# Row sums of the norms: one summed tile and two rounded products with ones in place of fp32 sums on TensorE

## The chip, the cores and the metric

One core of one Trainium2 chip runs the whole program. The metric is the device time of one execution in microseconds (us); runs are compared by their median. Five engines take part: TensorE (PE in the profile, with its weight loads as PEld), VectorE (DVE), ScalarE (ACT), GpSimd (POOL) and SyncE (SP), which issues the transfers.

## The reference

Two transformer blocks on a sequence of 256 tokens of 1024 features, batch 1. Only the normalisations matter here; each of them needs, for each token, a sum over the 1024 features:

```python
def rms_norm(x, g):
    xf = x.astype(jnp.float32)
    y = xf * lax.rsqrt(jnp.mean(xf * xf, axis=-1, keepdims=True) + EPS)
    return (y * g.astype(jnp.float32)).astype(x.dtype)

def layer_norm(x, g, b):
    mu = jnp.mean(xf, axis=-1, keepdims=True)
    var = jnp.mean(jnp.square(xf - mu), axis=-1, keepdims=True)
    y = (xf - mu) * lax.rsqrt(var + EPS)
    ...
```

The first block runs, with a residual after each: feed-forward 0, differential attention, feed-forward 1; then keys and values shared from a norm of their own; feed-forward 2, forgetting attention, feed-forward 3; and a final norm. The second block runs the convolution mixers (with one layer norm inside), cross-attention to a memory of 256 tokens (which has its own norm), and a mixture of experts called PEER. Each is preceded by an rms norm of the running x.

## The kernel before

x stays in SBUF transposed, `xT` [128, 8, 256]: features on the partitions in eight tiles (KT = 8), 256 tokens (T) along the free axis. A sum over features is therefore a sum over partitions and over eight tiles.

**Projections.** Every weight matrix streams through SBUF in pieces of 128x1024. A piece lands in `raw`, ACT rounds it to `whi` (L115), DVE makes the rest `wlo` (L116); there are four `whi`/`wlo` buffers. The activations are split the same way into `hi` and `lo`, and each product is three rounded (fp32r) matmuls into one bank, hi with hi, lo with hi and hi with lo (`mm3`, L147 to L149). One piece is 24 matmuls of 256 columns.

**Norm sums.** `Stat.add` squares a tile on ACT (L182). For most norms POOL adds the first seven squares (`sqa`, L193), and TensorE adds that sum and the eighth square over the partitions with fp32 matmuls against ones (L177), which leaves the sum for each token on the partitions, [128, 2]. With `on_pe=True` (memory, the first x norm, the layer norm) TensorE takes all eight squares one by one. `rstd` makes the root (ACT, L198) and the reciprocal (DVE, L199) on those two columns, and `along_row` (L215, two fp32 products with the identity) spreads the result along the tokens on all partitions, in the bank `pt`. ACT copies it to SBUF (`row_s`, L243).

**The pair.** The eight output tiles of a residual (L426) each feed a square and an unscaled `hi`/`lo` pair (`Norm.add`, L237 and L238). The first two weight pieces after a norm run on these unscaled tiles (`Norm.pair`, 48 matmuls into `mm` and `lg`), since they need no row; L257 multiplies the row in afterwards. In that time `scale` (L270 `nt` on DVE, `hi` on ACT, L275 `lo` on DVE; the form without shift uses L160 and L161) rescales the eight tiles. `fm_pair` then takes the next two pieces, k by k as the scaled tiles become ready.

**Order.** Each engine runs its list in order; a scheduler places what is independent. During feed-forward and attention a background task (ada rows: SP loads `araw`, DVE multiplies and sums it, L358) is spread over the same DVE list. In before.py each boundary between two parts is thus: last residual, row chain, `scale`, with weight splits and background work between them.

## Time and profile before

| | |
|---|---|
| median of 3 runs | 2267.92 us (2267.25 to 2269.08) |
| the profiled execution, own time | 2273.0 us |
| its span in the trace | 2271.2 us |
| PE busy | 2230.7 us, 98% of the span, 16748 matmuls |
| DVE busy | 1739.8 us, 77% |
| ACT busy | 1256.8 us, 55% |
| POOL busy | 75.5 us, 3% |
| mean granted clock | 0.995 |

The span is measured from the first to the last instruction; the execution's own time has 1.8 us around it. A busy share counts all stages alike, so what one boundary costs is to be read from the timeline there. The page counts each fp32 matmul of the program as several entries (the two L177 of one square are four entries).

### The profile page before, as it was taken

The page shows a single profiled execution, that of the slowest core. Times are in us where ns is not written, and L with a number is a line of the kernel's source. Part 1 is how long each engine was busy: PE and PEld are TensorE (multiplying, and loading weights), DVE is VectorE, ACT ScalarE, POOL GpSimd, SP SyncE. Part 2 cuts the span into 40 slices and gives each one's busy share as a digit, 9 for nine tenths or more (in the row PEclk, how much of TensorE's full clock was granted, in tenths as well). Part 3 has the DMA queues.
Part 4 walks back from the last instruction along what each step waited for, and adds up shares of the span by engine and source line. Part 5 has one row for each costly group of instructions (what it writes and reads, how often), then busy time and mean ns, then how long its engine had stood idle before and what let it go on. Part 6 is the DMA issues. An engine that isn't in the chain of part 4 may idle for free.

```text
span 2271.2 us, 42683 instructions
## 1 busy us (share of the span) xinstructions
PE 2230.7 (98%) x16748; PEld 2132.8 (94%) x16748; DVE 1739.8 (77%) x3503; ACT 1256.8 (55%) x2387; POOL 75.5 (3%) x80
## 2 busy tenths in 40 slices
PE   8989999999999999999999999999999999999998
PEld 8989998999999999999999999999999999888886
DVE  7757877977777787765799886899668997666665
ACT  5534487544654457545523555445567776555554
POOL 0000100000100020000100010000000000000000
PEclk9999999999999999999999999999999999999999
DMA  9787744777677763555444463355543434555554
GB/s 361 264 297 297 276 188 161 303 273 294 243 263 301 293 230 129 218 181 183 160 163 167 156 223 110 117 185 185 186 158 140 148 131 158 193 187 186 186 189 153
DMA packets 66185, 467.72 MB, mean 206 GB/s; under 512 B 7704, under 2 KB 7992, under 8 KB 10176
## 3 DMA queue, kind: packets, MB, share of 16 engines
q1 hardware_dynamic: 64608, 461.67, 55.3%
q0 software_dynamic: 1088, 2.81, 0.7%
q8 instruction: 132, 2.16, 0.4%
q14 instruction: 69, 0.57, 0.1%
q10 hardware_dynamic: 288, 0.52, 0.1%
HBM read 462.31 MB, written 2.62 MB: 205 GB/s over the span
## 4 chain that ended last, share of the span: by engine, by line
PE 91%; DVE 3%; ACT 3%; DMA 2%; issue 1%; POOL 0%; DVEq 0%; ACTq 0%; POOLq 0%
PE mm L149 22%; PE mm L147 22%; PE mm L148 22%; PE mm L1172 8%; PE lg L1172 8%; PE lg L1122 2%; PE mm L289 2%; DMA raw<-ffn_in 1%; PE po L177 1%; DVE wlo L116 1%; ACT whi L115 1%; DVE lo L238 0%; DVE lo L275 0%; ACT e L572 0%; PE po L958 0%
## 5 line engine op out<-in xcount | busy, mean ns | idle before, releaser
L115 ACT ACTIVATE whi<-raw 128x1024 fp32r<-128x1024 f32 x696 | 733.9, 1059 | 633.3 <-PE mm L148 401.1
L116 DVE TENSOR_TENSOR wlo<-raw,whi 128x1024 fp32r<-128x1024 f32 x696 | 851.3, 1228 | 296.8 <-ACT whi L115 294.9
L147 PE MATMUL mm<-hi,whi 128*128 128x256 f32 x3144 | 902.0, 287 | 9.8 <-ACT sil L450 9.2
L149 PE MATMUL mm<-hi,wlo 128*128 128x256 f32 x3144 | 894.2, 285 | 1.1 <-DVE wlo L116 0.8
L148 PE MATMUL mm<-lo,whi 128*128 128x256 f32 x3144 | 888.3, 283 | 0.1
L147 PEld LDWEIGHTS mm<-hi,whi 128*128 128x128 f32 x3144 | 597.1, 190 | 13.3 <-ACT sil L450 10.1
L149 PEld LDWEIGHTS mm<-hi,wlo 128*128 128x128 f32 x3144 | 597.9, 190 | 2.5 <-DVE wlo L116 2.2
L148 PEld LDWEIGHTS mm<-lo,whi 128*128 128x128 f32 x3144 | 598.4, 190 | 1.0 <-DVE lo L275 0.3
L149 PE MATMUL mm<-ghi,wlo 128*128 128x256 f32 x704 | 197.4, 280 | 0.0
L147 PE MATMUL mm<-ghi,whi 128*128 128x256 f32 x704 | 197.4, 280 | 0.0
L148 PE MATMUL mm<-glo,whi 128*128 128x256 f32 x704 | 197.4, 280 | 0.0
L358 DVE CUSTOM_DVE_ANT_0 araw<-araw,cb 128x1024 f32<-128x1024 f32 x160 | 190.4, 1219 | 4.3 <-DMA araw<-ada 3.3
L160 ACT ACTIVATE vph<-S 128x128 fp32r<-128x128 f32 x256 | 77.0, 302 | 130.7 <-PE lg L1172 130.6
L148 PEld LDWEIGHTS mm<-glo,whi 128*128 128x128 f32 x704 | 132.7, 188 | 0.0
L147 PEld LDWEIGHTS mm<-ghi,whi 128*128 128x128 f32 x704 | 132.7, 188 | 0.0
L149 PEld LDWEIGHTS mm<-ghi,wlo 128*128 128x128 f32 x704 | 132.6, 188 | 0.0
L161 DVE TENSOR_TENSOR vpl<-S,vph 128x128 fp32r<-128x128 f32 x256 | 73.4, 288 | 43.2 <-PE lg L1172 43.1
L820 DVE SCALAR_TENSOR_TENSOR cfc<-cf,vec,cfc 128x256 f32<-128x256 f32 x240 | 100.6, 502 | 0.0
L1114 DVE TENSOR_SCALAR ohA<-cst,sel 128x128 f32<-128x128 f32 x256 | 82.4, 343 | 21.7 <-PE lg L1122 20.7
L1172 PE MATMUL mm<-whi,vph 128*128 128x512 f32 x256 | 80.4, 395 | 0.2 <-ACT vph L160 0.2
L1172 PE MATMUL lg<-whi,vph 128*128 128x512 f32 x256 | 80.5, 395 | 0.0
L1172 PE MATMUL mm<-wlo,vph 128*128 128x512 f32 x256 | 80.5, 395 | 0.0
(389 smaller groups left out, 3269.1 us busy)
## 6 DMA issues: line engine op xcount, KB each, us to landing
raw<-ffn_in SPq DMA_DIRECT2D x88, 1024.0 KB, 5.0
araw<-ada SPq DMA_DIRECT2D x72, 1024.0 KB, 6.9
raw<-peer_u SPq DMA_DIRECT2D x64, 1024.0 KB, 4.8
raw<-peer_v SPq DMA_DIRECT2D x64, 1024.0 KB, 4.8
raw<-ffn_out SPq DMA_DIRECT2D x44, 1024.0 KB, 4.8
araw<-kv_ada SPq DMA_DIRECT2D x8, 1024.0 KB, 6.9
raw<-w_cf SPq DMA_DIRECT2D x8, 1024.0 KB, 4.8
raw<-w_scx SPq DMA_DIRECT2D x8, 1024.0 KB, 4.8
```

Source lines behind the costliest of these rows:

```text
L115: act.activation(hi[:, :m], r, AF.Copy)
L116: last_split[0] = dve.tensor_tensor(lo[:, :m], r, hi[:, :m], op=ALU.subtract)
L147: pe.matmul(o, a[0], b[0], start=start, stop=False)
L148: pe.matmul(o, a[0], b[1], start=False, stop=False)
L149: pe.matmul(o, a[1], b[0], start=False, stop=stop)
L160: act.activation(pair_hi, src, func, **kw)
L161: dve.tensor_tensor(pair_lo, src, pair_hi, op=ALU.subtract)
L289: pe.matmul(o, p[0][:, k * 128:(k + 1) * 128], h32[:, k, :], start=(k == 0), stop=(k == KT - 1))
L358: dve.tensor_tensor_reduce(out=raw[:, i, :], in0=raw[:, i, :], in1=cb, scale=1.0, scalar=0.0, op0=ALU.mult, op1=ALU.add, accum_out=acc[:, ...
L820: dve.scalar_tensor_tensor(o, cf[:, i, j:j + T], w, o, op0=ALU.mult, op1=ALU.add)
L1114: dve.tensor_scalar(A, iota, sel3[:, 0, t:t + 1], sel3[:, 2, t:t + 1], op0=ALU.is_equal, op1=ALU.mult)
L1172: pe.matmul(acc[t][d], lh, rh[:, d * 512:(d + 1) * 512], start=s0, stop=s1)
```

## The change

Every norm now adds all eight squares to one tile: POOL makes the first six adds, DVE the last (L187). That tile is split into a rounded `sqh` (ACT, L160) and the rest `sql` (DVE, L161), and two fp32r products, `ones_r` with each of them (L171, L172, 256 columns), leave the sum of each token on all 128 partitions at once, in `pt`. Root (ACT, L206) and reciprocal (DVE, L207) then run on the whole 128x256 row in SBUF, which `scale` and the other users read. `along_row` and the copy L243 are gone, and so is `on_pe`. The layer norm's mean takes the same way (`Sum`). The memory norm gets its per-token column back by two transposes. `rstd_after` (the norm of a normed x, before the convolutions) becomes the `of` argument. In the diff as shown blank lines are dropped.

```diff
     xT = xp.tile([128, KT, T], F32, name="xT")
-    ones0 = const.tile([128, 256], F32, name="ones0")
-    ones = ones0[:, 0:128]
+    ones = const.tile([128, 128], F32, name="ones")
+    ones_r = const.tile([128, 128], F32R, name="ones_r")
     eps_c = const.tile([128, 1], F32, name="eps_c")
-    dve.memset(ones0, 0.0)
     dve.memset(ones, 1.0)
+    dve.tensor_copy(ones_r, ones)
     dve.memset(eps_c, EPS)
...
-    class Stat:
-        def __init__(self, on_pe=False):
-            self.ps = bank("po", [128, 2, 128])
-            self.acc = None
-            self.k = 0
-            self.on_pe = on_pe
-        def sum(self, sq, first, last_):
-            for t in range(2):
-                o, b = (self.ps, ones0) if first and t == 0 else (self.ps[:, t, :], ones)
-                pe.matmul(o, sq[:, t * 128:(t + 1) * 128], b, start=first and t == 0,
-                          stop=last_ and t == 1, skip_group_check=True)
+    def over_features(src):
+        hi = work("sqh", [128, T], F32R, bufs=1)
+        lo = work("sql", [128, T], F32R, bufs=1)
+        split_into(hi, lo, src)
+        o = bank("pt", [128, T])
+        pe.matmul(o, ones_r, hi, start=True, stop=False)
+        pe.matmul(o, ones_r, lo, start=False, stop=True)
+        return o
+    class Sum:
+        def __init__(self):
+            self.acc, self.k = None, 0
+        def put(self, ap):
+            self.k += 1
+            if self.acc is None:
+                self.acc = ap
+                return
+            acc = work("sqa", [128, T], bufs=3)
+            (dve if self.k == KT else pool).tensor_tensor(acc, self.acc, ap, op=ALU.add)
+            self.acc = acc
+    class Stat(Sum):
...
             act.activation(sq, ap, AF.Square, scale=scale)
-            self.k += 1
-            if self.on_pe:
-                self.sum(sq, self.k == 1, self.k == KT)
-            elif self.k == KT:
-                self.sum(self.acc, True, False)
-                self.sum(sq, False, True)
-            elif self.acc is None:
-                self.acc = sq
-            else:
-                acc = work("sqa", [128, T], bufs=3)
-                pool.tensor_tensor(acc, self.acc, sq, op=ALU.add)
-                self.acc = acc
-        def rstd(self):
-            r = work("rstd", [128, 2], bufs=3)
-            act.activation(r, self.ps[:, :, 0], AF.Sqrt, scale=1.0 / D, bias=eps_c)
+            self.put(sq)
+        def row(self, r=None, scale=1.0, of=None):
+            r = const.tile([128, T], F32, tag="row", name="row", bufs=1) if r is None else r
+            o = over_features(self.acc)
+            if of is not None:
+                dve.tensor_tensor(r, o, of, op=ALU.mult)
+                dve.tensor_tensor(r, r, of, op=ALU.mult)
+                o = r
+            act.activation(r, o, AF.Sqrt, scale=1.0 / D, bias=eps_c)
             dve.reciprocal(r, r)
+            if scale != 1.0:
+                dve.tensor_scalar(r, r, scale, None, op0=ALU.mult)
             return r
-        def rstd_after(self, r1):
-            r = work("rstd", [128, 2], bufs=3)
-            dve.tensor_tensor(r, r1, r1, op=ALU.mult)
-            dve.tensor_tensor(r, self.ps[:, :, 0], r, op=ALU.mult)
-            act.activation(r, r, AF.Sqrt, scale=1.0 / D, bias=eps_c)
-            dve.reciprocal(r, r)
-            return r
-    def along_row(r):
-        o = bank("pt", [128, T])
-        for t in range(2):
-            pe.matmul(o[:, t * 128:(t + 1) * 128], r[:, t:t + 1].to_broadcast([128, 128]), ident,
-                      start=True, stop=True)
-        return o
...
-        def scaled_by(self, st, r=None, scale=1.0):
-            self.row = along_row(st.rstd() if r is None else r)
-            self.row_s = const.tile([128, T], F32, tag="row", name="row", bufs=1)
-            act.activation(self.row_s, self.row, AF.Copy, scale=scale)
+        def scaled_by(self, st, scale=1.0):
+            self.row = st.row(scale=scale)
             return self
...
                 t = work("nt", [128, T], bufs=3)
-                dve.tensor_tensor(t, oo[:, :T], self.row_s, op=ALU.mult)
+                dve.tensor_tensor(t, oo[:, :T], self.row, op=ALU.mult)
                 if self.b is not None:
...
-        def scale(self, keep=None, r=None):
-            row = self.row if r is None else along_row(r)
+        def scale(self, keep=None):
             for k in range(KT):
...
                 t = work("nt", [128, T], bufs=3) if keep is None else keep[:, k, :]
-                dve.scalar_tensor_tensor(t, xT[:, k, :], self.a[:, k:k + 1], row, op0=ALU.mult, op1=ALU.mult)
+                dve.scalar_tensor_tensor(t, xT[:, k, :], self.a[:, k:k + 1], self.row, op0=ALU.mult, op1=ALU.mult)
                 if self.b is None:
...
     hm = [memp.tile([128, KT, T], F32R, name=n) for n in ("mhi", "mlo")]
-    st = Stat(on_pe=True)
+    st = Stat()
     for k in range(KT):
...
     sync.dma_start(out=cb, in_=bass.AP(tensor=io["c"].tensor, offset=io["c"].offset, ap=[[0, 128], [1, D]]))
-    rm = st.rstd()
+    rm_row = st.row(memp.tile([128, T], F32, name="rm_row"))
     act.activation(cb, cb, AF.Silu)
-    rm_row = memp.tile([128, T], F32, name="rm_row")
-    act.activation(rm_row, along_row(rm), AF.Copy)
+    pt = bank("pt", [128, T])
+    rm = memp.tile([128, 2], F32, name="rm")
+    for t in range(2):
+        pe.transpose(pt[:, t * 128:(t + 1) * 128], rm_row[:, t * 128:(t + 1) * 128], ident)
+        dve.tensor_copy(rm[:, t:t + 1], pt[:, t * 128:t * 128 + 1])
...
-    st = Stat(on_pe=True)
+    st = Stat()
     for k in range(KT):
...
     norm = norm_of("0_sc1", "0_sh1")
-    norm.scale(r=st.rstd())
+    norm.scaled_by(st).scale()
     beside = prepare_bias()
...
     pool.memset(kA[64:66], 1.0)
-    r = st.rstd()
     with tc.tile_pool(name="kvp", bufs=1) as kp:
-        hk = norm.scaled_by(st, r).h
+        hk = norm.scaled_by(st).h
         fg = kp.tile([128, KT, 16], F32, name="fg")
...
+    row = norm.row
     norm = Norm(mod("1_sc1"), mod("1_sh1"), h=norm.h)
-    norm.scale(r=r)
+    norm.row = row
+    norm.scale()
     rate[0] = 0.6
...
-    r1 = st.rstd()
-    r12 = st2.rstd_after(r1)
-    dve.tensor_tensor(r12, r12, r1, op=ALU.mult)
+    rsk = ExitStack()
+    rp = rsk.enter_context(tc.tile_pool(name="rp", bufs=1))
+    r1 = st.row(rp.tile([128, T], F32, name="r1"))
+    norm.row = st2.row(of=r1)
+    dve.tensor_tensor(norm.row, norm.row, r1, op=ALU.mult)
...
         h32 = cp.tile([128, KT, T], F32, name="h32")
-        h = norm.scaled_by(st, r12).h
+        h = norm.h
         cf = cp.tile([128, KT, 288], F32, name="cf")
...
-        pm = bank("po", [128, T])
+        mean = Sum()
         for i in range(KT):
-            pe.matmul(pm, ones, cfc[:, i, :], start=(i == 0), stop=(i == KT - 1))
+            mean.put(cfc[:, i, :])
         mu = cp.tile([128, T], F32, name="mu")
-        act.activation(mu, pm, AF.Copy, scale=1.0 / D)
-        st = Stat(on_pe=True)
+        act.activation(mu, over_features(mean.acc), AF.Copy, scale=1.0 / D)
+        st = Stat()
         for i in range(KT):
...
             st.add(cfc[:, i, :])
-        r = along_row(st.rstd())
+        r = st.row()
         chi = cp.tile([128, KT, T], F32R, tag="phi", name="chi", bufs=2)
...
-        row = along_row(r1)
         for k in range(KT):
-            dve.scalar_tensor_tensor(xT[:, k, :], xT[:, k, :], v("final_g", k), row, op0=ALU.mult, op1=ALU.mult)
+            dve.scalar_tensor_tensor(xT[:, k, :], xT[:, k, :], v("final_g", k), r1, op0=ALU.mult, op1=ALU.mult)
         if tap:
...
         proj_fm(W, "w_mix_out", (mhi, mlo), lambda n, o: residual2(n, o, st, norm), wide=True)
+    rsk.close()
     if tap:
...
             t = ap_.tile([128, 256], F32, tag="qT", name="qT", bufs=4)
-            dve.tensor_tensor(t, o, norm.row_s, op=ALU.mult)
+            dve.tensor_tensor(t, o, norm.row, op=ALU.mult)
             qs[n] = t
```

What the scheduler makes of it is shown at three places. First DVE, from the last residual of feed-forward 0 to the first scaled tile of the attention's norm. L426 (L419 in the changed file) is the residual, L238 (L231) the unscaled `lo`, L270 (L260) `nt`, L275 (L265) the scaled `lo`. Before:

```order
L426 SCALAR_TENSOR_TENSOR xT<-mm,mod_gt_1285,xT 128x256
L116 TENSOR_TENSOR wlo<-raw,whi 128x1024
L238 SCALAR_TENSOR_TENSOR lo<-xT,mod_sc_2248,hi 128x256
L199 RECIPROCAL rstd<-rstd 128x2
L270 SCALAR_TENSOR_TENSOR nt<-xT,mod_sc_2248,pt 128x256 x3
L275 SCALAR_TENSOR_TENSOR lo<-nt,mod_sh_1767,hi 128x256 x3
L270 SCALAR_TENSOR_TENSOR nt<-xT,mod_sc_2248,pt 128x256 x3
L275 SCALAR_TENSOR_TENSOR lo<-nt,mod_sh_1767,hi 128x256
L270 SCALAR_TENSOR_TENSOR nt<-xT,mod_sc_2248,pt 128x256
L116 TENSOR_TENSOR wlo<-raw,whi 128x1024
L275 SCALAR_TENSOR_TENSOR lo<-nt,mod_sh_1767,hi 128x256 x3
```

Of the change:

```order
L419 SCALAR_TENSOR_TENSOR xT<-mm,mod_gt_1292,xT 128x256
L116 TENSOR_TENSOR wlo<-raw,whi 128x1024
L187 TENSOR_TENSOR sqa<-sqa,sq 128x256
L231 SCALAR_TENSOR_TENSOR lo<-xT,mod_sc_2255,hi 128x256
L161 TENSOR_TENSOR sql<-sqa,sqh 128x256
L207 RECIPROCAL row<-row 128x256
L260 SCALAR_TENSOR_TENSOR nt<-xT,mod_sc_2255,row 128x256 x3
L265 SCALAR_TENSOR_TENSOR lo<-nt,mod_sh_1774,hi 128x256 x2
L260 SCALAR_TENSOR_TENSOR nt<-xT,mod_sc_2255,row 128x256
L265 SCALAR_TENSOR_TENSOR lo<-nt,mod_sh_1774,hi 128x256
L260 SCALAR_TENSOR_TENSOR nt<-xT,mod_sc_2255,row 128x256 x2
L265 SCALAR_TENSOR_TENSOR lo<-nt,mod_sh_1774,hi 128x256 x3
L260 SCALAR_TENSOR_TENSOR nt<-xT,mod_sc_2255,row 128x256 x2
```

The last add, the split `sql` and the reciprocal of 256 columns stand in the list where the reciprocal of two columns stood, the add behind the weight split L116. The weight split that stood inside the scaling now follows behind it.

Second DVE, from the last residual of the attention to the first scaled tile of feed-forward 1. L358 (L348) is the background's product. Before:

```order
L426 SCALAR_TENSOR_TENSOR xT<-mm,mod_gt_2653,xT 128x256
L358 ISA araw,acc_gt_4541<-araw,cb 128x1024
L358 ISA acc_gt_4541 128x1
L238 SCALAR_TENSOR_TENSOR lo<-xT,mod_sc_4198,hi 128x256
L199 RECIPROCAL rstd<-rstd 128x2
L116 TENSOR_TENSOR wlo<-raw,whi 128x1024
L270 SCALAR_TENSOR_TENSOR nt<-xT,mod_sc_4198,pt 128x256 x3
L275 SCALAR_TENSOR_TENSOR lo<-nt,mod_sh_3323,hi 128x256 x3
L270 SCALAR_TENSOR_TENSOR nt<-xT,mod_sc_4198,pt 128x256 x3
L116 TENSOR_TENSOR wlo<-raw,whi 128x1024
```

Of the change:

```order
L419 SCALAR_TENSOR_TENSOR xT<-mm,mod_gt_2659,xT 128x256
L348 ISA araw,acc_gt_4546<-araw,cb 128x1024
L348 ISA acc_gt_4546 128x1
L187 TENSOR_TENSOR sqa<-sqa,sq 128x256
L231 SCALAR_TENSOR_TENSOR lo<-xT,mod_sc_4204,hi 128x256
L116 TENSOR_TENSOR wlo<-raw,whi 128x1024
L161 TENSOR_TENSOR sql<-sqa,sqh 128x256
L116 TENSOR_TENSOR wlo<-raw,whi 128x1024
L207 RECIPROCAL row<-row 128x256
L116 TENSOR_TENSOR wlo<-raw,whi 128x1024
L260 SCALAR_TENSOR_TENSOR nt<-xT,mod_sc_4204,row 128x256 x3
```

Three weight splits now stand ahead of the scaling, two of them between `sql` and the reciprocal and between the reciprocal and the first `nt`; before one did, behind the reciprocal.

Third DVE, at the norm of feed-forward 3's output ahead of the convolutions, where two sums are kept (x, and x weighted). `r_13168` is r1, the first row. Before:

```order
L238 SCALAR_TENSOR_TENSOR lo<-xT,gfm,hi 128x256
L199 RECIPROCAL rstd<-rstd 128x2
L205 TENSOR_TENSOR rstd<-rstd 128x2
L206 TENSOR_TENSOR rstd<-po,rstd 128x2
L208 RECIPROCAL rstd<-rstd 128x2
L788 TENSOR_TENSOR rstd<-rstd 128x2
L270 SCALAR_TENSOR_TENSOR h_13184<-xT,gfm,pt 128x256 x3
L161 TENSOR_TENSOR lo<-h_13184,hi 128x256 x3
```

Of the change:

```order
L187 TENSOR_TENSOR sqa<-sqa,sq 128x256
L231 SCALAR_TENSOR_TENSOR lo<-xT,gfm,hi 128x256
L187 TENSOR_TENSOR sqa<-sqa,sq 128x256
L161 TENSOR_TENSOR sql<-sqa,sqh 128x256 x2
L207 RECIPROCAL r_13168<-r_13168 128x256
L203 TENSOR_TENSOR row<-pt,r_13168 128x256
L204 TENSOR_TENSOR row<-row,r_13168 128x256
L116 TENSOR_TENSOR wlo<-raw,whi 128x1024 x2
L207 RECIPROCAL row<-row 128x256
L784 TENSOR_TENSOR row<-row,r_13168 128x256
L260 SCALAR_TENSOR_TENSOR h_13194<-xT,gfm,row 128x256 x3
```

Two reciprocals of 256 columns now follow one another, with two products and two weight splits between them, ahead of the first `h`.

## Rows read from the trace of the kernel before

**Rows 1.** The page: the chain that ended last, by engine, share of the span.
```profile
PE 91%; DVE 3%; ACT 3%; DMA 2%; issue 1%; POOL 0%; DVEq 0%; ACTq 0%; POOLq 0%
```

**Rows 2.** Groups by form, PE: line, engine, out<-in, shapes, count | busy us, mean ns | idle.
```profile
L177 PE MATMUL po<-ones,sq 128*128 128x128 f32 x126 | 18.9, 298 | 0.8 <-ACT sq L182 0.7
...
L215 PE MATMUL pt<-cst,rstd 128*128 128x128 f32 x52 | 8.5, 284 | 1.0 <-DVE rstd L199 1.0
...
L177 PE MATMUL po<-ones,sqa 128*128 128x256 f32 x18 | 5.7, 396 | 2.5 <-POOL sqa L193 2.5
...
L882 PE MATMUL po<-cfc,ones 128*128 128x256 f32 x16 | 3.6, 379 | 0.0
```

**Rows 3.** Timeline, the layer norm: start, us, engine, line, operation, out<-in, count.
```profile
1281.25 3.62 PE L882 MATMUL po<-cfc,ones 128*128 128x256 f32 x16
...
1286.25 4.05 PE L177 MATMUL po<-ones,sq 128*128 128x256 f32 x32
...
1294.00 1.08 DVE L894 TENSOR_TENSOR nt<-cfc,pt 128x256 f32<-128x256 f32 x3
```

**Rows 4.** Windows in the first feed-forward: busy us (count) by engine, then granted clock.
```profile
110.00:117.00 7.00, 7.00 (x60) 6.95 (x59) 1.18 (x2) 0.00 (x0) 0.00 (x0) 1.00 0.87 247
...
117.00:124.00 7.00, 0.19 (x3) 0.03 (x1) 0.32 (x1) 1.41 (x3) 0.00 (x0) 0.86 0.72 190
...
124.00:132.00 8.00, 8.00 (x48) 7.92 (x48) 4.74 (x7) 1.28 (x2) 0.93 (x1) 0.70 0.69 208
```

**Rows 5.** Groups by form, DVE: RECIPROCAL, then plain two-operand work, by width.
```profile
L744 DVE RECIPROCAL sm<-sm 128x2 f32<-128x2 f32 x16 | 2.5, 161 | 1.4 <-ACT e L742 1.1
...
L577 DVE RECIPROCAL rs<-sm 128x4 f32<-128x4 f32 x8 | 1.4, 172 | 0.0
...
L1076 DVE RECIPROCAL gs<-gs 128x8 f32<-128x8 f32 x2 | 0.4, 202 | 0.1
...
L233 DVE TENSOR_TENSOR lo<-mod_sh,hi 128x16 fp32r<-128x16 f32 x5 | 0.9, 173 | 0.3 <-ACT hi L232 0.3
...
L161 DVE TENSOR_TENSOR glo<-pr,ghi 128x256 fp32r<-128x256 f32 x88 | 36.7, 419 | 0.2 <-issue 0.2
```

**Rows 6.** Groups by form, POOL and ACT: adds of squares; the copy of the row.
```profile
L193 POOL TENSOR_TENSOR sqa<-sqa,sq 128x256 f32<-128x256 f32 x45 | 45.7, 1016 | 165.6 <-ACT sq L182 138.7 <-issue 25.8 <-POOL sqa L193 0.7
...
L243 ACT ACTIVATE row<-pt 128x256 f32<-128x256 f32 x8 | 3.1, 385 | 10.3 <-PE pt L215 10.3
```

**Rows 7.** Timeline, DVE, first feed-forward to attention.
```profile
275.24 0.48 DVE L426 SCALAR_TENSOR_TENSOR xT<-mm,mod_gt,xT 128x256 f32<-128x256 f32 x1 [0.55 <-PE mm L149]
...
276.27 1.23 DVE L116 TENSOR_TENSOR wlo<-raw,whi 128x1024 fp32r<-128x1024 f32 x1 [0.55 <-ACT whi L115]
...
279.18 1.26 DVE L270 SCALAR_TENSOR_TENSOR nt<-xT,mod_sc,pt 128x256 f32<-128x256 f32 x3 [1.22 <-ACT row L243]
...
283.79 1.23 DVE L116 TENSOR_TENSOR wlo<-raw,whi 128x1024 fp32r<-128x1024 f32 x1
...
287.25 0.49 DVE L275 SCALAR_TENSOR_TENSOR lo<-nt,mod_sh,hi 128x256 fp32r<-128x256 f32 x1
```

**Rows 8.** Timeline, DVE, attention to second feed-forward.
```profile
399.59 0.47 DVE L426 SCALAR_TENSOR_TENSOR xT<-mm,mod_gt,xT 128x256 f32<-128x256 f32 x1
...
399.99 1.21 DVE L358 CUSTOM_DVE_ANT_0 araw<-araw,cb 128x1024 f32<-128x1024 f32 x1
...
403.06 1.26 DVE L270 SCALAR_TENSOR_TENSOR nt<-xT,mod_sc,pt 128x256 f32<-128x256 f32 x3
```

**Rows 9.** Timeline, DVE, last feed-forward to convolutions.
```profile
1108.17 0.48 DVE L426 SCALAR_TENSOR_TENSOR xT<-mm,mod_gt,xT 128x256 f32<-128x256 f32 x1 [0.60 <-PE mm L149]
...
1113.29 1.26 DVE L270 SCALAR_TENSOR_TENSOR h<-xT,gfm,pt 128x256 f32<-128x256 f32 x3 [1.22 <-ACT row L243]
...
1117.96 1.43 DVE L161 TENSOR_TENSOR lo<-h,hi 128x256 fp32r<-128x256 f32 x4
```

**Rows 10.** Timeline, DVE, the start.
```profile
13.15 2.36 DVE L116 TENSOR_TENSOR wlo<-raw,whi 128x1024 fp32r<-128x1024 f32 x2 [0.46 <-ACT whi L115]
```

## The prediction

> **What bounds the kernel now.** I read the page first: TensorE carries 91% of the chain that ended last, DVE and ACT 3% each, transfers 2% [rows 1]. So microseconds taken off TensorE's list are worth their length, but only where TensorE is not about to wait for something else. The places where it does wait are the boundaries between parts, where a new norm needs its row. There I read the timeline boundary by boundary, with one question: when is the first scaled tile ready (L270), when the last (L275), and what stands between residual and row on DVE's list. The forecast is a replay of that list with the changed order, at each boundary, until the next weight piece after the scaled pair can run.
>
> **What leaves TensorE.** L177 and L215 at 128 columns stand 126 + 18 + 52 = 196 times on the page's count; 24 entries of L177 (one first entry of two for each of 12 groups of sums) and the 16 of L882 have 256 columns [rows 2]. In the layer norm 32 entries of L177 took 4.05 us, 0.127 each, and 16 of L882 3.62 us, 0.226 each [rows 3]. 196 x 0.127 + 40 x 0.226 = 33.9 us. A rounded matmul of 256 columns takes 7.00 / 60 = 0.117 us [rows 4]; 26 of them and four transposed entries come in, 3.5 us. If everything else were hidden, the kernel would be 30.4 us faster. That is the upper bound of the gain.
>
> **The price of the new row chain.** The expensive newcomer is the RECIPROCAL on 128x256, which no row of before shows. On 2, 4 and 8 columns it takes 161, 172 and 202 ns: 5.5 and 7.5 ns for each further element, where a subtraction goes from 173 ns on 16 columns to 419 on 256, 1.0 ns for each [rows 5]. Lower bound: it behaves as the subtraction, 0.42 us. Upper: 202 + 248 x 7.5 = 2.06 us. I take 6.25 ns, 1.75 us, because all three rows of the same operation show the steep slope. The other steps: last add and `sql` 0.42 each [rows 5], `sqh` and the root 0.39 each by the copy of the row [rows 6], two products 0.12 each. Serially 0.42 + 0.39 + 0.42 + 0.12 + 0.39 + 1.75 = 3.5 us, and some 0.05 to 0.1 us between engines. The Trainium skill, "VectorE: DVE Perf Modes", section "First, the fixed hardware budget", says that the reciprocal is an iterative divide with a repeat count of 8, and its table has the engine at 0.96 GHz. If that is eight cycles for each element, it gives an estimate of 2.1 us, and the sum below would be some 3 us higher; the rows' 7.5 ns lean that way.
>
> **Feed-forward 0 to attention: +1.6.** Before, the residual ends at 275.72, L116 holds DVE from 276.27 to 277.50, the first scaled tile starts at 279.18 and the last `lo` ends at 287.74 [rows 7]. Of the change, the add stands behind L116: 277.5 to 277.85; `sqh` to 278.35, `sql` to 278.85, products, root to 279.75, reciprocal to 281.5. The scaling starts 2.3 us later. The L116 that stood inside it (283.79, 1.23 [rows 7]) now stands behind, so the last `lo` is only 1.2 later. But that weight split is what the third piece waits for: it ends at about 290.2, where TensorE finished the scaled pair near 288.5 before. Some 48 x 0.117 = 5.6 us of unscaled matmuls cover the chain; what the pair loses of L177 and L215 (1.7 us) makes its cover end earlier and gains nothing here, because the scaling sets the end.
>
> **Attention to feed-forward 1: +3.2.** Residual and background L358 stand as before (399.59, 399.99, to 401.20 [rows 8]). Then add, `lo`, L116, `sql`, L116, reciprocal, L116, each 1.23 for the splits: first scaled tile at about 407.4 instead of 403.06 [rows 8]. One split leaves the scaling again (-1.1): +3.2, with TensorE idle for about 3.5 us.
>
> **Four more boundaries of this pattern**, replayed alike: feed-forward 1 to keys and values, with two L358 in the chain, +2.2; feed-forward 2 to forgetting attention, +1.3; that to feed-forward 3, +1.2 (there TensorE waited before for POOL's last add, and no longer does); cross-attention to PEER, where nothing stands on DVE's list, -0.5. Keys and values to feed-forward 2 loses its second L215, -0.4. The cross-attention norm scales nothing, 0.
>
> **Feed-forward 3 to convolutions: +4.4.** Two sums, and the second row needs the first. Before, residual at 1108.17, scaled tiles from 1113.29, the last `lo` ends at 1119.39 [rows 9]. Now a reciprocal, two products, two L116 (their `whi` waits for buffers that the pair frees) and a second reciprocal: first tile at about 1120.1, 6.8 later; that the scaling has fewer waits of its own and the next splits are already made gives some 2.4 back. TensorE would idle some 6 us. **The clock, +2.2.** In feed-forward 0 it ran 60 matmuls in 7.00 us, then worked 0.19 us of 7.00, and then made only 48 in 8.00 at a mean granted clock of 0.70 [rows 4]: 48 x 0.117 = 5.6, so 2.4 us lost to the lower of the two levels, 1.2 GHz. I charge that once, behind the longest new wait.
>
> **Layer norm: -3.9.** L882 (3.62), L177 (4.05) and four entries of L215 (4 x 0.127) go, 8.2 us; four products, 0.5, come. The squares now take six POOL adds of 1.02 [rows 6], which TensorE must await where it summed each square as it came: about 3.2 us more waiting, and 0.6 for two splits. -8.2 + 0.5 + 3.2 + 0.6 = -3.9. The mean's adds follow tiles that the convolution makes one by one and stay hidden.
>
> **Start: +3.8.** The memory norm's squares were summed as they landed; now six POOL adds follow one another, and the `sql` and the long reciprocal stand among the first weight splits (13.15, 2.36 for two [rows 10]). Those slip by about 2.3 us, the x norm's by a little more; L177 x32 and two L215 leave TensorE. Between 0 (all under transfers) and 5.5.
>
> **Sum.** 3.8 + 1.6 + 3.2 + 2.2 - 0.4 + 1.3 + 1.2 + 4.4 + 2.2 - 3.9 - 0.5 = +15.1 us. The profiled execution took 2273.0, 1.8 of it outside the span, and stands 5.1 above the median of 2267.9; with the change it would take 2288, and the median 2283.
>
> **The rivals.**
> *The chain is hidden.* The pair's cover (5.6 us) holds a chain of 3.5, the scheduler's order costs nothing, and TensorE's saving counts. For it: 91% of the chain is TensorE's. Against it: the scaling, eight tiles at roughly 1 us each, ended after the pair already, at 287.74 [rows 7], so its start decides. All hidden gives 2237.5, half of the boundaries 2253. Chance 0.12.
> *The reciprocal is cheap*, 0.42 us. Then each of seven boundary chains (eight reciprocals) and the start are about 1.3 shorter, 9 x 1.3 = 12, and the convolution boundary's idle falls too short for the clock, 2.2: +1, or 2269, no change. Chance 0.12.
> *The clock falls at every new wait.* TensorE would idle 2 to 4 us at two more boundaries and in the layer norm. At 2.2 to 2.4 each: +5 to +7, 2288 to 2290; with the upper price of the reciprocal (0.3 x 9) up to 2293. Chance 0.22. The Trainium skill, "TensorE: Matmul & The Clock Gate", section "HAM oscillation", describes a kernel that re-throttles at every wait between groups; the row after the idle 7 us agrees, and rows for waits of 3 us are missing.
> *The start is absorbed*: the first stage may be bound by transfers, so +3.8 becomes 0, 2279. That lies inside the likeliest case.
>
> **How the numbers follow.** The likeliest, replay with the 1.75 us reciprocal, has 0.54: 2283, and 2276 to 2288 with its own bounds. A measurement of this kernel tells 0.2%, 4.5 us, from no change, so faster is below 2263.4 and slower above 2272.5. Faster gets the hidden chain, 0.12; same the cheap reciprocal and a little of the likeliest, 0.13; slower 0.75. The range 2260 to 2295 leaves out most of the hidden chain and a little above.
>
> **What would show it.** RECIPROCAL L207 at 1.6 to 2.1 us; L260 first at a boundary 2 to 4 us later after the residual than L270 was; new idle time of TensorE before scaled tiles, the longest, about 6 us, ahead of the convolutions with a lower clock behind it; from the mean's end to the scaled layer norm fewer microseconds of TensorE. It is wrong if L207 takes near 0.4 us, if TensorE's waits at the boundaries are no longer than before, or if the weight splits between the steps turn out to start earlier than I let them.

## The result and the profile after

The changed kernel took 2293.02 us in the median of 4 runs (2292.02 to 2295.68), the kernel before 2268.30 beside it: ratio 1.0106, 95% interval 1.0094 to 1.0118. That is 24.7 us slower where 15.1 were forecast; it lies inside the range, near its upper end. The profiled execution took 2295.68, 2.7 above the median; that of before stood 5.1 above its own, so the traces differ by 22.7 us where the medians differ by 24.7.

The page of the changed kernel: the span, busy time by engine, and the chain that ended last.

```profile
span 2293.9 us, 42338 instructions
PE 2216.1 (97%) x16540; PEld 2113.5 (92%) x16540; DVE 1770.9 (77%) x3532; ACT 1260.2 (55%) x2391; POOL 99.2 (4%) x104
PE 87%; DVE 5%; ACT 4%; issue 2%; DMA 1%; POOL 0%; DVEq 0%; SPq 0%; ACTq 0%; POOLq 0%
```

TensorE's busy time fell by 14.6 us (2230.7 before), the span grew by 22.7. So some 37 us of new idle time stand on the engine that bounds the kernel, and its share of the chain fell from 91% [rows 1] to 87%, where DVE's and ACT's rose.

The new row chain, groups by form of the changed kernel (busy us, mean ns of one, then the idle time ahead):

```profile
L207 DVE RECIPROCAL row<-row 128x256 f32<-128x256 f32 x10 | 17.5, 1748 | 4.0 <-ACT row L206 4.0
L187 DVE TENSOR_TENSOR sqa<-sqa,sq 128x256 f32<-128x256 f32 x12 | 6.3, 527 | 10.3 <-POOL sqa L187 9.7 <-ACT sq L195 0.6
L161 DVE TENSOR_TENSOR sql<-sqa,sqh 128x256 fp32r<-128x256 f32 x13 | 5.5, 421 | 1.9 <-ACT sqh L160 1.6
L206 ACT ACTIVATE row<-pt,eps_c 128x256 f32<-128x256 f32 x9 | 4.2, 471 | 8.4 <-PE pt L172 8.4
L171 PE MATMUL pt<-sqh,ones_r 128*128 128x256 f32 x13 | 4.8, 371 | 12.6 <-ACT sqh L160 12.2
```

The reciprocal takes 1.748 us, as the slope of [rows 5] gave. The last row holds 12.2 us in which TensorE stands before the first of the two products: 4.16 at the start, 3.77 in the layer norm, where the forecast had such a wait, and 1.34 to 1.47 at three boundaries, which I had not counted. There the product lies in the list among the unscaled matmuls, and those behind it wait too.

First boundary, feed-forward 0 to attention, DVE's timeline of the changed kernel:

```profile
276.45 0.48 DVE L419 SCALAR_TENSOR_TENSOR xT<-mm,mod_gt,xT 128x256 f32<-128x256 f32 x1 [0.47 <-PE mm L149]
277.49 1.23 DVE L116 TENSOR_TENSOR wlo<-raw,whi 128x1024 fp32r<-128x1024 f32 x1 [0.55 <-ACT whi L115]
278.63 0.42 DVE L187 TENSOR_TENSOR sqa<-sqa,sq 128x256 f32<-128x256 f32 x1
...
279.53 0.43 DVE L161 TENSOR_TENSOR sql<-sqa,sqh 128x256 fp32r<-128x256 f32 x1
280.96 1.75 DVE L207 RECIPROCAL row<-row 128x256 f32<-128x256 f32 x1 [1.00 <-ACT row L206]
282.75 1.28 DVE L260 SCALAR_TENSOR_TENSOR nt<-xT,mod_sc,row 128x256 f32<-128x256 f32 x3
...
288.63 0.90 DVE L265 SCALAR_TENSOR_TENSOR lo<-nt,mod_sh,hi 128x256 fp32r<-128x256 f32 x2
...
290.17 1.22 DVE L116 TENSOR_TENSOR wlo<-raw,whi 128x1024 fp32r<-128x1024 f32 x1
```

The residual stands 1.21 us later than in [rows 7] (276.45 against 275.24). Less that shift, the reciprocal starts at 279.75, the scaling at 281.54 and the weight split behind it at 288.96: all three within 0.1 us of the replay. The last `lo` ends 0.6 us later than before, where the replay had 1.2.

Second boundary, attention to feed-forward 1, DVE's timeline:

```profile
402.90 0.47 DVE L419 SCALAR_TENSOR_TENSOR xT<-mm,mod_gt,xT 128x256 f32<-128x256 f32 x1
...
406.64 1.21 DVE L116 TENSOR_TENSOR wlo<-raw,whi 128x1024 fp32r<-128x1024 f32 x1
407.78 1.74 DVE L207 RECIPROCAL row<-row 128x256 f32<-128x256 f32 x1
409.44 1.15 DVE L116 TENSOR_TENSOR wlo<-raw,whi 128x1024 fp32r<-128x1024 f32 x1
410.52 1.26 DVE L260 SCALAR_TENSOR_TENSOR nt<-xT,mod_sc,row 128x256 f32<-128x256 f32 x3
```

The first scaled tile comes 7.62 us after the residual's start, 3.47 before [rows 8]: 4.15 later, 4.3 in the replay. What the replay had not priced stands behind it. Windows of the changed kernel, at this boundary and ahead of the convolutions (busy us and count of PE, PEld, DVE, ACT, POOL, then the granted clock, the transfers' share and GB/s):

```profile
406.00:412.00 6.00, 2.79 (x22) 2.59 (x21) 6.00 (x9) 3.46 (x6) 0.00 (x0) 0.93 0.57 218
412.00:420.00 8.00, 8.00 (x46) 7.85 (x46) 8.00 (x21) 2.61 (x6) 0.00 (x0) 0.63 0.32 132
1126.00:1133.50 7.50, 1.35 (x10) 1.14 (x9) 7.29 (x11) 3.19 (x5) 0.00 (x0) 0.85 0.40 140
1133.50:1140.00 6.50, 6.50 (x37) 6.32 (x37) 6.50 (x19) 4.26 (x9) 0.00 (x0) 0.64 0.13 53
```

TensorE ran at the lower of its two levels, 1.2 GHz, for part of the stretch behind each of these waits. At 0.117 us a matmul, 46 would take 5.4 of the 8.00 us and 37 would take 4.3 of 6.50: 2.6 and 2.2 us. I had charged the second and left the first to a rival.

Ahead of the convolutions, DVE's timeline, and under it TensorE's first matmul on scaled tiles:

```profile
1120.32 0.48 DVE L419 SCALAR_TENSOR_TENSOR xT<-mm,mod_gt,xT 128x256 f32<-128x256 f32 x1 [0.58 <-PE mm L149]
...
1124.96 1.75 DVE L207 RECIPROCAL r<-r 128x256 f32<-128x256 f32 x1
...
1127.68 2.36 DVE L116 TENSOR_TENSOR wlo<-raw,whi 128x1024 fp32r<-128x1024 f32 x2
1129.96 1.75 DVE L207 RECIPROCAL row<-row 128x256 f32<-128x256 f32 x1
...
1132.20 1.28 DVE L260 SCALAR_TENSOR_TENSOR h<-xT,gfm,row 128x256 f32<-128x256 f32 x3
```

```profile
1133.18 0.80 PE L147 MATMUL mm<-hi,whi 128*128 128x256 f32 x2 [6.15 <-ACT hi L160]
```

Less the shift of 12.15 us, the first tile stands at 1120.05 (1120.1 in the replay), and the wait is 6.15 us.

The layer norm, POOL's timeline and then TensorE's:

```profile
1306.38 2.02 POOL L187 TENSOR_TENSOR sqa<-sq 128x256 f32<-128x256 f32 x1 [6.26 <-ACT sq L195]
1308.47 4.81 POOL L187 TENSOR_TENSOR sqa<-sqa,sq 128x256 f32<-128x256 f32 x5
```

```profile
1314.24 0.39 PE L171 MATMUL pt<-sqh,ones_r 128*128 128x256 f32 x1 [3.77 <-ACT sqh L160]
```

Six adds end at 1313.28, then one on DVE and the rounding; TensorE stands for 3.77 us in front of its product. Behind this wait, too, the granted clock fell. The first row below is the stretch from the product on; the second is the same stretch of e11, a kernel of the next section in which TensorE does not wait here:

```profile
1314.20:1322.00 7.80, 7.75 (x52) 7.76 (x53) 4.80 (x9) 4.18 (x5) 0.00 (x0) 0.78 0.38 134
1310.90:1318.70 7.80, 7.80 (x68) 7.80 (x67) 6.61 (x10) 6.43 (x8) 0.00 (x0) 1.00 0.76 271
```

At 0.117 us a matmul, 52 would take 6.1 of the 7.75 us: some 1.7 us are lost, at a granted clock of 0.78 against 1.00.

**Where the time went, by stage.** For each instruction of DVE and ACT that both traces have (same tiles, same place in the sequence) I took the difference of its end times; the median over the 14 us that end a stage says how late the kernel is there, and the difference of two such medians what the stage cost. All in us against the trace of the kernel before; the columns e1 to e12 belong to the next section.

```
stage                      forecast after   e1    e2    e3    e7    e9   e10   e11   e12
start and ff 0                 3.8    1.7   1.1   1.7  -2.2  -2.4  -4.6  -4.1   0.0   2.9
ff 0 to attention              1.6    1.6   0.2   7.9   2.9   0.5   0.7   1.4   1.6   0.6
attention to ff 1              3.2    3.8   0.6   8.5   4.7   0.0   1.8   3.6   2.8   2.2
ff 1 to k/v to ff 2            1.8    1.4   2.1   6.9   8.2   0.3   0.7   1.0   1.4   2.9
ff 2 to forgetting att.        1.3    2.9   3.0   8.7   5.0   1.6  -0.7   2.9   3.0   3.1
that to ff 3                   1.2    0.9  -0.1   6.8   2.2   0.1   2.2   2.0   0.9   1.7
ff 3 to convolutions           6.6    7.9   3.5  14.9   8.4   1.4   0.0   7.9   7.8   1.9
convolutions, layer norm      -3.9   -1.1   3.0   0.1   3.9   2.8   0.0  -0.1  -6.7   4.5
cross-attention norm           0.0    0.3  -0.9   8.4  -0.8  -0.5   0.3  -0.8   0.3   0.7
cross-attention to PEER       -0.5    2.8  -0.2   4.5   3.1   1.1   1.0   0.7   1.0  -0.1
sum                           15.1   22.3  12.3  68.5  35.4   4.9   1.4  14.4  12.2  20.3
without the first row         11.3   20.6  11.1  66.8  37.6   7.3   6.0  18.5  12.2  17.4
```

The first row is no measure of the change: e9 leaves the start as before and stands 4.6 us earlier there. From the second boundary on, stages that are alike in two kernels mostly agree within a few tenths. The exceptions are attention to feed-forward 1 (3.8 in the changed kernel, 2.8 in e11) and cross-attention to PEER (2.8 and 1.0). The code there is the same, and so are TensorE's waits (3.21 and 3.19 us, 1.09 and 1.10); what differs is the granted clock behind them. Rows of the changed kernel, then of e11, behind the second of these waits:

```profile
1455.50:1459.00 3.50, 3.12 (x14) 3.15 (x15) 2.80 (x13) 1.24 (x4) 0.00 (x0) 0.51 0.60 201
1447.20:1450.70 3.50, 3.10 (x26) 3.13 (x27) 3.31 (x16) 1.26 (x4) 0.00 (x0) 1.00 0.68 204
```

12 matmuls fewer are some 1.4 us. So a stage that holds such a wait is known to 1 or 2 us from one trace, not better.

### The profile page after: what moved, and what is told of

The parts are those of the page before. It is cut to its first block, busy times and chain, and to the rows that moved or that the text cites. A ratio compares the mean times of both kernels' runs of the same rounds, so it can differ in the third digit from the quotient of the medians.

```text
span 2293.9 us, 42338 instructions
## 1 busy us (share of the span) xinstructions
PE 2216.1 (97%) x16540; PEld 2113.5 (92%) x16540; DVE 1770.9 (77%) x3532; ACT 1260.2 (55%) x2391; POOL 99.2 (4%) x104
## 4 chain that ended last, share of the span: by engine, by line
PE 87%; DVE 5%; ACT 4%; issue 2%; DMA 1%; POOL 0%; DVEq 0%; SPq 0%; ACTq 0%; POOLq 0%
PE mm L149 21%; PE mm L147 21%; PE mm L148 21%; PE mm L1168 8%; PE lg L1168 8%; PE lg L1118 2%; PE mm L279 2%; DVE wlo L116 1%; ACT whi L115 1%; DMA raw<-ffn_in 1%; DVE cfc L816 1%; DVE araw L348 0%; POOL sqa L187 0%; DVE lo L231 0%; DVE row L207 0%
## 5 line engine op out<-in xcount | busy, mean ns | idle before, releaser
L116 DVE TENSOR_TENSOR wlo<-raw,whi 128x1024 fp32r<-128x1024 f32 x696 | 850.0, 1225 | 285.7 <-ACT whi L115 283.8
L348 DVE CUSTOM_DVE_ANT_0 araw<-araw,cb 128x1024 f32<-128x1024 f32 x160 | 190.9, 1221 | 3.1 <-DMA araw<-ada 2.8
L160 ACT ACTIVATE vph<-S 128x128 fp32r<-128x128 f32 x256 | 77.2, 302 | 131.8 <-PE lg L1168 131.7
L161 DVE TENSOR_TENSOR vpl<-S,vph 128x128 fp32r<-128x128 f32 x256 | 73.3, 288 | 43.6 <-PE lg L1168 43.5
L1168 PE MATMUL lg<-whi,vpl 128*128 128x512 f32 x256 | 80.6, 395 | 0.0
```

Of the source, the lines that this page charges most:

```text
L116: last_split[0] = dve.tensor_tensor(lo[:, :m], r, hi[:, :m], op=ALU.subtract)
L160: act.activation(pair_hi, src, func, **kw)
L161: dve.tensor_tensor(pair_lo, src, pair_hi, op=ALU.subtract)
L348: dve.tensor_tensor_reduce(out=raw[:, i, :], in0=raw[:, i, :], in1=cb, scale=1.0, scalar=0.0, op0=ALU.mult, op1=ALU.add, accum_out=acc[:, ...
L1168: pe.matmul(acc[t][d], lh, rh[:, d * 512:(d + 1) * 512], start=s0, stop=s1)
```

## The experiments

Two theories stood against each other. One: the chain of the row on DVE, above all the reciprocal of 256 columns, sets the start of the scaled tiles. The other: the chain is covered, and the time goes to the order of the weight splits or to squares on POOL. Medians in us; before is 2268.1 to 2269.2 beside all of them.

**e1, without the reciprocal.**

```diff
-            dve.reciprocal(r, r)
+            dve.tensor_scalar(r, r, 0.0, 0.25, op0=ALU.mult, op1=ALU.add)
```

> The changed kernel, but the reciprocal of the 128x256 row (1.75 us) is replaced by one multiply and add that sets the row to 0.25, so the normalisation is left out. Theory (the row chain on DVE sets the start of the scaled tiles): each of eight boundary reciprocals gives back 1.4 us where the scaling is late, 8 x 1.4 = 11, the start about 1, and the idle 6 us ahead of the convolutions falls under 4, so its lower clock goes, 2: 2277 to 2281 us. Rival (the order of the weight splits and the squares on POOL cost the time, the reciprocal lies behind them): 2289 to 2293 us.

Measured 2284.35, ratio 1.0065 (1.0048 to 1.0082). The reciprocals are worth 8.7 us of the 24.7 by the medians, 9.5 by the stages. The seven stages at boundaries together gave back 12.2 (1.4 + 3.2 - 0.7 - 0.1 + 1.0 + 4.4 + 3.0), near the theory's 11 and 2, but the layer norm got 4.1 us worse, so the sum stayed short of the expectation. TensorE waited 6.12 us there, as DVE took up the subtractions, behind weight splits, 4.0 us after ACT had begun to write the mean (1.7 in the changed kernel). Ahead of the convolutions the wait fell from 6.15 to 2.16 us, but the lower clock did not go: 0.72 in the stretch 1124 to 1130 us.

**e2, the reciprocal three times.**

```diff
             dve.reciprocal(r, r)
+            dve.reciprocal(r, r)
+            dve.reciprocal(r, r)
```

> The changed kernel with the reciprocal taken three times (1/(1/(1/x))), 3.5 us more in each of the 12 row chains. Theory: 8 boundary chains, each fully exposed, 28 us, the layer norm 3.5, and a lower clock behind more of the waits, 2 to 8: 2325 to 2333 us. Rival (hidden): under 2305 us.

Measured 2342.01, ratio 1.0324 (1.0306 to 1.0341), 49 us more than the changed kernel and above even the theory's 2325 to 2333. The first five boundaries lost 4.7 to 6.3 us more than in the changed kernel for 3.5 us of added chain; behind the longer waits the clock was lower. Windows of e2 from the pair of the first boundary on:

```profile
276.00:286.00 10.00, 6.73 (x55) 6.32 (x53) 7.86 (x10) 4.66 (x7) 2.47 (x8) 0.95 0.69 272
286.00:296.00 10.00, 6.65 (x33) 6.51 (x33) 10.00 (x24) 3.87 (x9) 0.00 (x0) 0.54 0.31 108
```

In the second window 33 matmuls took 6.65 us, 0.20 each, at a granted clock of 0.54. The layer norm took 1.2 us of it (0.1 against -1.1), so its reciprocal is mostly covered; the cross-attention norm, free with one, cost 8.4.

**e3, the chain ahead of the splits.** The third and fourth split after a norm are queued behind the reciprocal.

```diff
-            dve.reciprocal(r, r)
+            hold[:] = [dve.reciprocal(r, r), 2]
...
+            hold[1] -= 1
+            with after(hold) if -2 <= hold[1] < 0 else nullcontext():
+                last_split[0] = dve.tensor_tensor(lo[:, :m], r, hi[:, :m], op=ALU.subtract)
```

> The changed kernel with the third and fourth weight split after a norm, and so the background products, queued on DVE behind the row's reciprocal. Theory: at attention to feed-forward 1 two splits (2.4 us), at feed-forward 1 to keys and values one product of the background (1.2), ahead of the convolutions two splits (2.4) leave the chain; the splits come later by as much, and half of it is lost again to the next piece: 2287 to 2290 us. Rival (the sum of DVE's work between residual and last scaled tile decides, not its order): 2292 to 2295 us.

Measured 2313.18, ratio 1.0202 (1.0185 to 1.0219), 20 us more than the changed kernel. Both expectations fell. TensorE's waits of the changed kernel and then of e3 for `lo` and `wlo`, by the weight loads:

```profile
L148 PEld LDWEIGHTS mm<-lo,whi 128*128 128x128 f32 x3144 | 600.5, 191 | 4.9 <-DVE lo L265 1.9
L149 PEld LDWEIGHTS mm<-hi,wlo 128*128 128x128 f32 x3144 | 600.1, 191 | 4.0 <-DVE wlo L116 3.4
```

```profile
L151 PEld LDWEIGHTS mm<-lo,whi 128*128 128x128 f32 x3144 | 601.4, 191 | 6.6 <-DVE lo L268 4.2 <-DVE lo L164 1.4
L152 PEld LDWEIGHTS mm<-hi,wlo 128*128 128x128 f32 x3144 | 601.0, 191 | 4.5 <-DVE wlo L118 4.2
```

The held splits landed behind the reciprocal: one ahead of the first scaled tile at each of the first two boundaries, two ahead of the convolutions, and a second one at the first boundary between the first `nt` and the first `lo`. There they delay the scaled tiles, and the pieces came later besides. The splits that stood in the gaps of the chain, which I had priced as waits, were not a cost that a better order removes in this way. What makes up all 20 us was not taken apart.

**e4, two columns again but for the second row ahead of the convolutions.** The edit is like that of e7 below, but the second row ahead of the convolutions, which needs the first, keeps the wide way. The kernel also left out the factor of 1/16 of the cross-attention norm's row.

> The changed kernel with root and reciprocal on two columns again: the one summed tile goes unsplit through two fp32 products (four entries), root and reciprocal on 128x2, then the spread along the row and a copy to SBUF as before. Only the second row ahead of the convolutions keeps the wide way. Theory: split (0.8) and long reciprocal (1.6) go, spread and copy with their hand-overs come (1.2), so each of 8 chains is about 1.2 us shorter and the clock ahead of the convolutions stays: 2279 to 2283 us; still above the kernel before, because the last add stands on DVE behind a weight split. Rival (the saved TensorE entries count where the chain is short): 2262 to 2268 us.

Measured 2280.82, ratio 1.0058 (1.0041 to 1.0075), within the theory's figure. By its trace, taken as in the table, it lost 9.5 us behind the first row of the table, 7.3 of them at the one boundary that kept a wide row, with one wide reciprocal.

**e5, the layer norm the old way; e6, the start the old way.** In each the old `Stat` with its fp32 sums stands beside the new one, under the name `OldStat`.

```diff
-        mean = Sum()
+        pm = bank("po", [128, T])
         for i in range(KT):
-            mean.put(cfc[:, i, :])
+            pe.matmul(pm, ones, cfc[:, i, :], start=(i == 0), stop=(i == KT - 1))
...
-        st = Stat()
+        st = OldStat(on_pe=True)
```

> The changed kernel with the layer norm's mean and sum of squares taken the old way (16 entries of L882, 32 of L177, rstd, spread). In the traces the changed layer norm gave back 1.2 us where the prediction had 3.9. If the trace is read rightly: 1 to 2 us slower than the changed kernel, 2294 to 2295 us. If the 3.9 was right and another stage hid it: 2296 to 2298 us.

> The changed kernel with the memory norm and the first x norm taken the old way (each square on TensorE). The prediction gave the start 3.8 us; the traces show TensorE 5.4 us late at 90 us and 3.0 at 145, behind a wait for transfers. If what is left behind that wait counts: 3 us faster than the changed kernel, 2290 us. If the transfers set the time there anyway: 2292 to 2294 us.

e5: 2293.3, ratio 1.0111 (1.0094 to 1.0128), no difference that these runs can tell; by the stages it stands within 0.4 us of the kernel before there, against -1.1, so the new way gained about 1 us and not 3.9. e6: 2300.0, ratio 1.0136 (1.0119 to 1.0153), 7 us slower, on neither expectation. Its trace has the boundaries of the changed kernel (20.7 without the first row) and one long wait in feed-forward 0, which ACT's timeline names:

```profile
110.60 1.06 ACT L116 ACTIVATE whi<-raw 128x1024 fp32r<-128x1024 f32 x1 [14.75 <-DMA raw<-ffn_in]
```

ACT idles 14.75 us until a weight piece has landed, and TensorE behind it. Where such waits fall differs between all the kernels here, those with the same start too, so what the change costs at the start stays open.

**e7, two columns in every norm.**

```diff
+            po = bank("po", [128, 2, 128])
+            for t in range(2):
+                pe.matmul(po[:, t, :], self.acc[:, t * 128:(t + 1) * 128], ones, start=True, stop=True)
...
+            act.activation(c, o, AF.Sqrt, scale=1.0 / D, bias=eps_c)
+            dve.reciprocal(c, c)
...
-            o = over_features(self.acc)
...
-            act.activation(r, o, AF.Sqrt, scale=1.0 / D, bias=eps_c)
-            dve.reciprocal(r, r)
...
+            act.activation(r, along_row(self.cols() if c is None else c), AF.Copy, scale=scale)
```

> All norms with one summed tile and two fp32 products, root and reciprocal on two columns, also ahead of the convolutions, where the earlier kernel of this kind still had two wide reciprocals and lost 5.8 us by its trace. Theory (the wide reciprocal is what costs): that boundary falls to about +1, so 2270 to 2277 us, of the size of the kernel before. Rival (the last add on DVE costs there as much as the reciprocal): 2278 to 2281 us.

Measured 2275.14, ratio 1.0028 (1.0018 to 1.0037). The boundary ahead of the convolutions fell from 7.9 to 1.4 us, as the theory has it. The expectation speaks of two wide reciprocals in e4, but its trace has one: leaving the first row's wide chain out took 0.6 us off there (7.9 to 7.3), the second row's 5.9. 17.9 of the 24.7 us are gone; only one summed tile, its add on DVE, and the layer norm's new sums are left.

**e8, the kernel before with the start's squares on POOL.**

```diff
-    st = Stat(on_pe=True)
+    st = Stat()
```

> The kernel before, with the memory norm and the first x norm summed on POOL as its other norms are. In the trace of the two-column kernel the start was 2.9 us earlier than before. If that comes from the squares that leave TensorE: 2264 to 2266 us; if from the order of the first weight splits alone: 2267 to 2269 us.

Measured 2273.1, ratio 1.0020 (1.0010 to 1.0030): not faster, though the squares there left TensorE's list but for one sum and the last; on neither expectation.

**e9, the wide reciprocal alone.** In the kernel before, at six norms:

```diff
+            if r is None:
+                c = work("rstd", [128, 2], bufs=3)
+                act.activation(c, st.ps[:, :, 0], AF.Copy)
+                act.activation(self.row_s, along_row(c), AF.Sqrt, scale=1.0 / D, bias=eps_c)
+                dve.reciprocal(self.row_s, self.row_s)
...
```

> The kernel before with one part of the change alone: at six norms (five with scaled tiles, and the cross-attention's) the raw sums are spread along the row first, and root and reciprocal run on 128x256; sums, adds and the other norms stay as they were. Theory (the wide reciprocal on DVE delays the scaled tiles): 5 x 1.6 = 8 us plus the clock at one or two waits, 2276 to 2281 us beside a before of 2268. Rival (it is hidden behind the unscaled pair): 2268 to 2270 us.

Measured 2274.45, ratio 1.0024 (1.0015 to 1.0033), 5.5 us, between the two: 8 or more by the theory, at most 2 by the rival. One operation of 1.75 us in place of 0.16 costs 1.1 us on average at each of the five boundaries with scaled tiles when sums and adds stay as they were.

**e10, without the split.**

```diff
-        hi = work("sqh", [128, T], F32R, bufs=1)
-        lo = work("sql", [128, T], F32R, bufs=1)
-        split_into(hi, lo, src)
...
-        pe.matmul(o, ones_r, hi, start=True, stop=False)
-        pe.matmul(o, ones_r, lo, start=False, stop=True)
+        pe.matmul(o, ones, src, start=True, stop=True)
```

> The changed kernel with the summed tile unsplit: one fp32 product with ones (four entries or their like on TensorE) in place of sqh, sql and two rounded products. Theory (the chain on DVE and ACT sets the time): 0.42 + 0.39 and two hand-overs leave each of 8 boundary chains, TensorE gets 0.6 more in its covered time: 1 us each, 2284 to 2287 us. Rival (the splits lie beside other work and TensorE's 13 x 0.6 counts): 2293 to 2300 us.

Measured 2289.87, ratio 1.0098 (1.0084 to 1.0112), 3.2 us less than the changed kernel, between the two expectations, and the intervals overlap. By the stages 2.1 behind the first row, as much as the last boundary alone has, where the granted clock stayed at 1.00 in e10.

**e11, the layer norm's squares added on DVE.**

```diff
-        st = Stat()
+        st = Stat(dve)
...
-            (dve if self.k == KT else pool).tensor_tensor(acc, self.acc, ap, op=ALU.add)
+            (dve if self.k == KT else self.eng).tensor_tensor(acc, self.acc, ap, op=ALU.add)
```

> The changed kernel with the layer norm's seven adds of squares on DVE (0.42 each) in place of six on POOL. In the changed kernel TensorE waits 3.9 us for the first of the two products there. Theory (that wait is for POOL's adds, 1.0 us each): DVE takes 6 x 0.42 = 2.5 of work beside the subtractions that it makes anyway (8 x 0.35), the sum is ready about 2 us earlier and the wait falls to some 2 us: 2290 to 2292 us, and by position in the trace 2 us less in this stage. Rival (the wait is for the squares on ACT and the table load): no difference in this stage, 2292 to 2294 us.

Measured 2287.37, ratio 1.0078 (1.0064 to 1.0092), 5.7 us less than the changed kernel, and 5.6 less in this stage, nearly three times what the theory had: the whole wait of 3.77 us went, not a part of it, and with it the lower clock behind it. TensorE's product in e11, without a wait:

```profile
1310.95 0.28 PE L171 MATMUL pt<-sqh,ones_r 128*128 128x256 f32 x1
```

**e12, e7 with the last add on POOL.**

```diff
-            (dve if self.k == KT else pool).tensor_tensor(acc, self.acc, ap, op=ALU.add)
+            pool.tensor_tensor(acc, self.acc, ap, op=ALU.add)
```

> The kernel with all norms on two columns (2275 us), with the last add on POOL too. Theory (what it still loses against the kernel before is the last add, which queues behind a weight split on DVE): POOL's add takes 1.0 us instead of 0.42 but waits for nothing, so at the boundaries where a split stands ahead (0.5 to 1.2 us of waiting) it is even or 0.5 us better each: 2271 to 2275 us. Rival (the length of the add itself counts): 0.6 us more at each of 8 boundaries, 2278 to 2281 us.

Measured 2288.84, ratio 1.0083 (1.0070 to 1.0097), 13.7 more than e7. The theory fell; the rival's sign is right, its size too small. POOL's add of 1.0 us stands behind the add before it on the same engine, where DVE's took 0.42; and at three boundaries where e7 has a granted clock of 1.00, e12 has 0.72 to 0.74 over some 6 us.

## Why the prediction was right, and where its sizes were off

**The upper bound of the gain** was no gain: TensorE's busy time fell by 14.6 us, not by 30.4 (in part because matmuls at the lower clock take longer), and came back as waits. The page's busy shares could not show that; the timelines did.

**The price of the chain** held: 1.748 us against 1.75, 6.2 ns for each element beyond eight. That it fits so closely is luck: slopes of 5.5 and 7.5 ns allowed 1.57 to 2.06. The upper bound of 2.06 was too high. So was the estimate of 2.1 us from the Trainium skill, "VectorE: DVE Perf Modes", section "First, the fixed hardware budget"; the measurement decides.

**The replay of DVE's list** held to 0.2 us at the three boundaries shown above. e1, e2, e7 and e9 change only the chain's length or form, and the time follows. So the mechanism stands, and the boundary to the attention cost 1.6 us as forecast.

**The clock was mis-sized**, and it is the largest term that was. It was charged once, 2.2 us ahead of the convolutions. It fell at three more places: 2.6 us at attention to feed-forward 1, some 1.7 in the layer norm and some 1.4 at cross-attention to PEER, by the windows above. All three had stood only with the rival, which had +5 to +7 us for two more boundaries and the layer norm, and 5.7 came: it was the better forecast. Only its "every" is wrong, and the length of the last wait does not decide alone. Behind waits of 1.12, 2.07 and 1.07 us (the first boundary, keys and values, feed-forward 3) the changed kernel has a granted clock of 1.00, but behind 1.09 us at PEER it has 0.51. At keys and values, the changed kernel after 2.07 us and e1 after 2.14:

```profile
606.00:616.00 10.00, 8.97 (x67) 8.30 (x68) 10.00 (x26) 6.63 (x16) 0.00 (x0) 1.00 0.01 2
601.30:608.00 6.70, 6.47 (x40) 6.27 (x41) 6.70 (x22) 3.90 (x8) 0.00 (x0) 0.75 0.01 2
```

Attention to feed-forward 1 still came out at 3.8 for 3.2; what gave the rest back was not taken apart.

**Layer norm: -3.9 was wrong, -1.1 measured.** The terms that failed are the clock, put at nothing there, the splits, and to a lesser part the wait. The first product waits 3.77 us where I had 3.2; `sql` of the mean, behind a weight split on DVE, holds TensorE for 1.12 where I had 0.6 for all splits; and the lower clock costs some 1.7. -8.2 + 0.5 + 3.8 + 1.1 + 1.7 = -1.1. e11, which moves the adds of the squares to DVE, takes the wait and the clock away, and -8.2 + 0.5 + 1.1 = -6.6 stands beside its measured -6.7. The wait itself is not six equal adds of 1.02 us: the first took 2.02 us beside DVE's subtractions, the last four 0.72 each, and the three buffers of the squares let ACT go only as fast as POOL.

**The mean's adds do not stay hidden from DVE.** In the changed kernel five of DVE's eight `cfc<-cf,vec` products run beside one of POOL's adds of the mean for most of their time, and these five take 0.81 to 0.88 us. In e5, which sums the mean on TensorE, all eight take 0.41 to 0.42. Rows of the changed kernel and of e5 (ns of the shortest, the median and the longest):

```profile
L814 DVE TENSOR_SCALAR cfc<-cf,vec x8: 404/818/883, 1142.5 to 1263.5; 128x256 f32<-128x256 f32 x8
L875 DVE TENSOR_SCALAR cfc<-cf,vec x8: 406/411/421, 1140.2 to 1259.5; 128x256 f32<-128x256 f32 x8
```

DVE's last tiles of the convolution, compared as in the table, are 1.6 us later than TensorE's list ahead of them, and not later in e5. What of that reaches the end was not separated.

**Cross-attention to PEER: -0.5 was wrong, +2.8 measured.** Some 1.4 us of it is the lower clock, which e11 does not have there: its 1.0 is what the rest costs. For that rest I priced the chain and not the splits behind it, which I had priced at the first boundary. Before, two `whi` stood on ACT and the first `wlo` on DVE inside the scaling; of the change, the profile has both `wlo` behind the last scaled tile. ACT and DVE of the kernel before, then DVE of the changed one:

```profile
1430.61 1.99 ACT L115 ACTIVATE whi<-raw 128x1024 fp32r<-128x1024 f32 x2
1432.23 1.22 DVE L116 TENSOR_TENSOR wlo<-raw,whi 128x1024 fp32r<-128x1024 f32 x1
```

```profile
1452.80 1.09 DVE L161 TENSOR_TENSOR lo<-nt,hi 128x256 fp32r<-128x256 f32 x3
...
1454.47 2.35 DVE L116 TENSOR_TENSOR wlo<-raw,whi 128x1024 fp32r<-128x1024 f32 x2
```

**Feed-forward 2 to the forgetting attention: +1.3 was too small, 2.9 measured.** e1 has 3.0 without the reciprocal and e10 has 2.9 without the split of the summed tile, so it is neither alone. What it is was not settled; two columns with the same add (e7) cost 1.6.

**The rival "the reciprocal is cheap"** gave no change; e1 without any price for it still stands 16 us above before. What it leaves (the add on DVE, the split, the hand-overs, the wait for the products in TensorE's list, the layer norm) is more than the reciprocal's own 8.7 us, and I had taken it as small beside it. Two columns with the same add (e7) stand 5.9 above before, so the wide chain is most of the 24.7 us, and its reciprocal about half of that chain.

**The sum.** Sign and mechanism are right, the size is not: 15.1 us forecast, 24.7 measured. Nearly all terms that were off were too small, so they did not cancel, and the range held only by its upper end, which stood for the rivals.

## What to carry to other kernels

An operation moved from two columns to 256 is priced by its own slope, not by that of its neighbours: three widths of it in the old trace bounded the reciprocal to 1.57 to 2.06 us, where its neighbours' slope had 0.42. Work taken off the bounding engine pays only where that engine has a list to go on with; at a boundary, follow the chain to the first tile and to the last, and then to whatever was queued behind it. A product that waits for a late operand also holds the ready ones behind it. A wait that the lower clock follows costs twice, and here that happened behind waits of 1.1 to 6.2 us at some boundaries and not at others, so look at the granted clock behind each. Here e7 and e11 each took back a part, but none of the kernels run beats the one before; both together were not run.
